# Deferring the gate columns of an input projection: one sample group or three

## The chip, the cores and the metric

The kernel runs on one core of one Trainium2 chip. The metric is the time of one execution on the device in microseconds (us), the median over several runs; lower is better. One further execution is taken with the hardware profiler, and all rows below come from it.

## The reference

One layer of a bidirectional encoder is applied to a prompt of 256 tokens and to a sample of 2048 tokens, all in float32 with a model width of 1024. The part that matters here:

```python
h = _rmsnorm(x, prm['norm_mix'][l])
p = h @ prm['w_in'][l]
pg, pr, ps = _split(p, [GLA_COLS, RWKV_COLS, SSD_COLS])
o_gla = _gla_mixer(pg, ...)
o_rwkv = _rwkv7_mixer(pr, ...)
o_ssd = _ssd_mixer(ps, ...)
mix = jnp.concatenate([o_gla, o_rwkv, o_ssd], axis=-1)
x = x + mix @ prm['w_out'][l]
h = _rmsnorm(x, prm['norm_ffn'][l])
x = x + (jax.nn.silu(h @ prm['ffn_gate'][l]) * (h @ prm['ffn_up'][l])) @ prm['ffn_down'][l]
```

Each of the three token mixers runs a scan forward over the tokens and a second one backward, and sums them. Two of them end with a gate: the first multiplies by `silu(g)`, where `g` is 256 columns of `p`, and the third by `silu(z)`, where `z` is 512 columns of `p`. No scan needs these 768 columns. They are the gate columns of this text.

## The kernel before, in words

**Tiling.** Tokens are handled in groups of 512 (`GS`) for dense work and in blocks of 256 (`TB`) for the mixers. The prompt is one group of one block. The sample is four groups, called group 0 to group 3 here, that start at tokens 256, 768, 1280 and 1792 of the joint axis.

**The projection.** `in_proj` makes one group's columns of `p` and stores them to DRAM. It begins with `normed`, which calls `norm_T` for each of the four 128-token tiles: one DMA loads the rows into a tile `x` (two buffers), ScalarE squares them, VectorE works out the inverse root and scales, TensorE transposes in eight steps of 128 x 128, and ScalarE and VectorE split the result into a high and a low part. These are the two tiles `hT0` and `hT1`, of which there is one buffer each. `normed` runs at a raised priority (`high_priority(offset=3000)`). Then follow the steps of `in_proj`, with a `yield` behind each: four of `in_chan` for the RWKV columns, one for small columns, four for the SSD convolution channels, one for the GLA queries and keys, one of `in_tok` for the GLA values. `in_gates` makes the gate columns in three more steps: one `in_chan` (256 columns, result by channel, matmuls with 512 tokens moving) and two `in_tok` (256 columns each, result by token, 256 columns moving). Each step loads a weight panel of 1024 x 256 in four DMAs on SP's queue, splits it into a high part on ScalarE and a low part on VectorE or GpSimd (`panel`), and multiplies three times per tile of the contraction (`acc3`: high by high, high by low, low by high).

`in_proj` has a flag `part`: 2 makes all columns, 0 leaves the gate columns out, 1 makes the gate columns alone. With 1 the whole `normed` is done again, since `hT` has been overwritten by then.

**The passes.** `pass_a` is the forward scan of one block (and what the backward one can be given in advance), nine in all. `first(end)` emits those first passes whose inputs are there. `pass_b` is the backward scan of one block and needs the gate columns of its block: it reads `d_gl` and `d_z` from DRAM. `second(t0, n)` emits a group's second passes from the last block to the first, each followed by `out_proj`. `ffn` is the feed-forward of one group and needs `hT` again.

**Order.** `run` writes the order of emission out by hand, and a scheduler then orders the instructions of each engine by this order (as priority) and a simulated timeline. Work that is emitted later fills an engine where earlier work isn't ready. Inside one engine instructions run in the order found. In `run`, for each sample group: the projection without gate columns, the first passes that have become possible, then the group's gate steps. Group 0 leaves its gate steps out, and these are made behind the loop. Then come two steps of the prompt's `ffn`, and then, going from group 3 down to group 0, second passes and `ffn` in alternation. `order` is the list of sample groups from the last to the first.

The line that the change touches in the loop, and the two behind it:

```python
dense = self.in_proj(t0, n, 2 if k or len(sample) == 1 else 0)
...
if len(sample) > 1:
    emit(self.in_proj(*sample[0], 1))
```

Of the kernel before, what the change touches and what calls it, by code (L numbers as in the profile page):

```python
# [69 lines left out]
class Encoder:  # L70
# [1029 lines left out]
    def run(self):  # L1100
        self.setup()
        prompt = [(t, min(GS, self.Lp - t)) for t in range(0, self.Lp, GS)]
        sample = [(t, min(GS, self.NT - t)) for t in range(self.Lp, self.NT, GS)]
        done, st, sb, self.rs2, self.ready = 0, None, None, {}, {}

        def first(end):

            nonlocal done, st
            while done < self.NB:
                lo, hi = self.seq(done)  # L1110
                need = (done + 1) * TB
                if need > end or (need == end and need != hi):
                    break
                if done * TB == lo:
                    st = self.states()
                self.pass_a(done, st)
                done += 1

        def second(t0, n):

            nonlocal sb
            mix = None
            for b in range((t0 + n) // TB - 1, t0 // TB - 1, -1):
                if (b + 1) * TB == self.seq(b)[1]:
                    sb = self.states()
                if mix is not None:
                    self.out_proj(b + 1, mix)
                mix = self.pass_b(b, sb)
                self.free = False
                yield  # L1130
            self.out_proj(t0 // TB, mix)

        def run(*steps):

            steps = list(steps)
            while steps:
                for s, k in list(steps):
                    for _ in range(k):
                        if next(s, steps) is steps:
                            steps.remove((s, k))  # L1140
                            break

        def emit(steps, k=None):
            while (k is None or k > 0) and next(steps, steps) is not steps:
                k = k and k - 1

        order = sample[::-1]
        self.last = order[0][0]
        for t0, n in prompt:
            emit(self.in_proj(t0, n))  # L1150
            if t0 == 0:
                self.setup_mixers()
            first(t0 + n)
        ahead = [second(*g) for g in reversed(prompt)]
        for k, (t0, n) in enumerate(sample):
            dense = self.in_proj(t0, n, 2 if k or len(sample) == 1 else 0)
            if k == 1 or k == len(sample) - 1:
                for s in ahead:
                    emit(s, 1)
                    emit(dense, 5)  # L1160
                    emit(s)
                ahead = []
                first(t0)
            if k > 0 or len(sample) == 1:
                emit(dense, 11)
                first(t0 + n)
            emit(dense)
        if len(sample) > 1:
            emit(self.in_proj(*sample[0], 1))
        early = [self.ffn(*g, inside=g[1] <= TB) for g in prompt]  # L1170
        for f in early:
            emit(f, 2)
        rest = [self.ffn(*g, after) for g, after in zip(order, order[1:] + [None])]
        for k, f in enumerate(early + rest):
            steps = [(second(*order[k]), 1)] if k < len(order) else []
            run(*steps, (f, 2))
# [30 lines left out]
```

## Time and profile before

| What | us |
|---|---|
| median of 3 runs | 3870.42 |
| lowest and highest run | 3868.07, 3875.63 |
| the profiled execution, its own time | 3868.33 |
| its span in the trace | 3866.6 |

The span reaches from the first to the last instruction of the program. TensorE's matmuls are called PE in the profile, its weight loads PEld, VectorE is DVE, ScalarE is ACT, GpSimd is POOL and SyncE, on whose queue most DMAs are issued, is SP. The granted clock (PEclk) is TensorE's clock as a share of full speed. Matmuls are pipelined, and their ends in the trace are modelled, so the time from one start to the next is the better measure for a row of equal matmuls. In a row of a group, "mean ns" is that of one instruction.

### The profile page before, as it was taken

How to read it: one execution, taken by the hardware profiler on the slowest of the kernel's cores; microseconds unless marked ns; L12 is line 12 of the kernel's file. 1: busy time of each engine (PE TensorE's matmuls, PEld its weight loads, DVE VectorE, ACT ScalarE, POOL GpSimd, SP SyncE). 2: the span in 40 equal slices, each digit the busy share in tenths (PEclk: the TensorE clock that was granted, in tenths of full speed). 3: DMA queues.
4: the chain of work that ended last, by engine and by line, in shares of the span. 5: the costliest groups of instructions: out<-in, count | busy, mean ns of one | idle time of the engine just before them, and what ended most of it. 6: DMA issues, size and time to landing. Idle time of an engine off the chain costs nothing.

```text
span 3866.6 us, 74228 instructions
## 1 busy us (share of the span) xinstructions
PE 3670.0 (95%) x28958; PEld 3100.1 (80%) x28958; DVE 2414.1 (62%) x5551; ACT 1488.2 (38%) x3354; POOL 614.3 (16%) x636
## 2 busy tenths in 40 slices
PE   6899899899989988999999999999999999999998
PEld 6777677667767767798978888888888888888887
DVE  5943486776884788677756564574654755545444
ACT  4533253544553454443433232333233332333222
POOL 3321123342432332211000000010000000000000
PEclk9999899999989989999999999999999999999999
DMA  6543343333334432555544333434343442434232
GB/s 179 165 142 112 95 151 118 105 121 112 118 98 116 134 104 92 159 158 169 179 149 136 108 122 123 142 116 131 105 142 103 144 131 88 141 104 136 93 99 93
DMA packets 430190, 486.44 MB, mean 126 GB/s; under 512 B 49345, under 2 KB 389457, under 8 KB 428689
## 3 DMA queue, kind: packets, MB, share of 16 engines
q1 hardware_dynamic: 390720, 422.40, 35.8%
q10 hardware_dynamic: 38112, 55.65, 4.0%
q8 instruction: 228, 3.74, 0.4%
q0 software_dynamic: 1008, 3.67, 0.3%
q14 instruction: 122, 0.99, 0.1%
HBM read 395.42 MB, written 86.18 MB: 125 GB/s over the span
## 4 chain that ended last, share of the span: by engine, by line
PE 78%; DVE 12%; DMA 5%; ACT 2%; issue 2%; POOL 0%; SPq 0%; ACTq 0%; DVEq 0%; POOLq 0%
PE d L116 48%; PE g L116 15%; PE s L116 7%; PE a L116 4%; PE c L116 3%; DVE mix L102 2%; DMA mix<-d_xb 1%; DVE wl L92 1%; DVE mix L92 1%; PE d L362 1%; ACT mix L105 1%; DMA b<-d_rk 1%; DMA x<-d_x 0%; DVE b9x L102 0%; PE s L587 0%
## 5 line engine op out<-in xcount | busy, mean ns | idle before, releaser
L116 PE MATMUL d<-hT,wh 128*128 128x512 f32 (+3 forms) x4384 | 1268.0, 374 | 6.2 <-ACT ev L109 2.5
L109 ACT ACTIVATE wh<-wr 128x512 fp32r<-128x512 f32 (+1 forms) x1084 | 624.0, 621 | 981.9 <-PE d L116 587.1
L116 PEld LDWEIGHTS d<-hT,wh 128*128 128x128 f32 (+1 forms) x4384 | 786.8, 191 | 156.9 <-issue 10.8
L92 DVE TENSOR_TENSOR wl<-wr,wh 128x512 fp32r<-128x512 f32 x944 | 646.6, 712 | 360.8 <-ACT wh L109 354.4
L116 PE MATMUL d<-hT,wl 128*128 128x512 f32 (+3 forms) x2192 | 812.1, 374 | 13.1 <-DVE wl L92 13.1
L116 PEld LDWEIGHTS d<-hT,wl 128*128 128x128 f32 (+1 forms) x2192 | 416.0, 190 | 92.1 <-DVE wl L92 15.1
L116 PE MATMUL g<-hT,wh 128*128 128x512 f32 x896 | 284.5, 394 | 0.2 <-ACT hT L109 0.2
L92 POOL TENSOR_TENSOR wl<-wr,wh 128x512 fp32r<-128x512 f32 (+1 forms) x140 | 209.7, 1500 | 451.6 <-ACT wh L109 350.9
L116 PE MATMUL d<-wh,b 128*128 128x256 f32 x928 | 266.8, 289 | 2.4 <-DVE b4d L92 2.0
L116 PE MATMUL d<-wh,hT 128*128 128x256 f32 x1216 | 253.4, 299 | 12.8 <-ACT wh L109 5.9
L116 PE MATMUL d<-wl,b 128*128 128x256 f32 x928 | 260.5, 282 | 0.0
L116 PE MATMUL d<-wh,b9x 128*128 128x256 f32 x928 | 259.5, 283 | 0.0
L116 PEld LDWEIGHTS d<-wh,hT 128*128 128x128 f32 x1216 | 201.7, 198 | 26.6 <-ACT wh L109 7.2
L116 PEld LDWEIGHTS g<-hT,wh 128*128 128x128 f32 x896 | 166.6, 188 | 35.3 <-ACT hT L109 0.5
L116 PE MATMUL d<-wl,hT 128*128 128x256 f32 x608 | 180.3, 298 | 11.5 <-DVE wl L92 11.3
L116 PEld LDWEIGHTS d<-wh,b 128*128 128x128 f32 x928 | 174.3, 188 | 8.9 <-DVE b4d L92 2.2
L116 PE MATMUL d<-wh,mix 128*128 128x256 f32 x832 | 169.8, 292 | 7.0 <-ACT mix L109 2.2
L116 PE MATMUL g<-hT,wl 128*128 128x512 f32 x448 | 175.4, 392 | 0.0
L116 PEld LDWEIGHTS d<-wl,b 128*128 128x128 f32 x928 | 174.8, 188 | 0.7
L116 PEld LDWEIGHTS d<-wh,b9x 128*128 128x128 f32 x928 | 174.0, 189 | 1.3
L102 DVE SCALAR_TENSOR_TENSOR mix<-mix,cwh,mix 128x256 f32<-128x256 f32 x288 | 136.3, 521 | 18.9 <-ACT mix L105 18.9
L116 PEld LDWEIGHTS d<-wh,mix 128*128 128x128 f32 x832 | 136.9, 195 | 10.0 <-ACT mix L109 2.9
(387 smaller groups left out, 6429.3 us busy)
## 6 DMA issues: line engine op xcount, KB each, us to landing
wr<-in_w_in SPq DMA_DIRECT2D x260, 256.0 KB, 3.2
wr<-in_ffn_gate SPq DMA_DIRECT2D x220, 256.0 KB, 2.9
wr<-in_ffn_up SPq DMA_DIRECT2D x220, 256.0 KB, 3.0
wr<-in_ffn_down SPq DMA_DIRECT2D x220, 256.0 KB, 2.9
wr<-in_w_out SPq DMA_DIRECT2D x144, 256.0 KB, 3.0
x<-in_x_sample SPq DMA_DIRECT2D x20, 512.0 KB, 3.7
x<-d_x SPq DMA_DIRECT2D x20, 512.0 KB, 4.3
q_s<-qs ACTq DMA_DIRECT2D x18, 520.0 KB, 4.4
```

Of the source, the lines that this page charges most:

```text
L92: (eng or self.nc.vector).tensor_tensor(out=out, in0=a, in1=b, op=op)
L102: (eng or self.nc.vector).scalar_tensor_tensor(out=out, in0=a, scalar=s, in1=b, op0=op0, op1=op1)
L105: self.nc.scalar.activation(out=out, in_=in_, func=f, **k)
L109: self.nc.scalar.activation(out=out, in_=in_, func=AF.Copy)
L116: self.nc.tensor.matmul(out, lhsT=lhsT, rhs=rhs, start=start, stop=stop, tile_position=tp, skip_group_check=lax)
L362: self.nc.tensor.transpose(ps[:, k * P:(k + 1) * P], h[:, (4 * q + k) * P:(4 * q + k + 1) * P], self.c["ident"])
```

## The change

The flag becomes 0 for all sample groups but the last. Behind the loop the gate columns of groups 2, 1 and 0 are made in this order, each with its own `normed`. Group 3's gate steps stay where they were, and so do those of the prompt.

```diff
         for k, (t0, n) in enumerate(sample):
-            dense = self.in_proj(t0, n, 2 if k or len(sample) == 1 else 0)
+            dense = self.in_proj(t0, n, 2 if k == len(sample) - 1 else 0)
             if k == 1 or k == len(sample) - 1:
@@
             emit(dense)
-        if len(sample) > 1:
-            emit(self.in_proj(*sample[0], 1))
+        for g in order[1:]:
+            emit(self.in_proj(*g, 1))
         early = [self.ffn(*g, inside=g[1] <= TB) for g in prompt]
```

## Rows read from the trace of the kernel before

**Rows 1.** The page: busy time and share of the span of each engine

```profile
PE 3670.0 (95%) x28958; PEld 3100.1 (80%) x28958; DVE 2414.1 (62%) x5551; ACT 1488.2 (38%) x3354; POOL 614.3 (16%) x636
```

**Rows 2.** The page: the chain that ended last, by engine

```profile
PE 78%; DVE 12%; DMA 5%; ACT 2%; issue 2%; POOL 0%; SPq 0%; ACTq 0%; DVEq 0%; POOLq 0%
```

**Rows 3.** Busy time by stage: length; PE, PEld, DVE, ACT, POOL; clock, DMA, GB/s

```profile
652.00:960.00 308.00, 291.93 (x2394) 224.01 (x2395) 214.78 (x476) 144.73 (x341) 103.81 (x102) 0.97 0.38 119
960.00:1304.00 344.00, 317.29 (x2597) 250.72 (x2597) 240.97 (x529) 152.63 (x356) 108.83 (x106) 0.95 0.38 117
1304.00:1562.00 258.00, 233.13 (x2230) 184.28 (x2229) 207.26 (x438) 135.89 (x320) 91.53 (x101) 0.93 0.32 101
1562.00:2000.00 438.00, 415.61 (x4494) 377.94 (x4493) 307.14 (x766) 184.92 (x439) 50.78 (x58) 0.97 0.54 168
2000.00:3866.00 1866.00, 1844.14 (x12892) 1599.34 (x12891) 1046.68 (x2415) 593.38 (x1255) 78.04 (x87) 1.00 0.38 118
```

**Rows 4.** SP's timeline: start, length, the last value stores of groups 1 to 3

```profile
652.22 0.42 SPq L407 DMA_DIRECT2D d_v<-ev  x1
...
960.08 9.72 SPq L407 DMA_DIRECT2D d_v<-ev  x4
...
1299.19 10.25 SPq L407 DMA_DIRECT2D d_v<-ev  x4
```

**Rows 5.** TensorE's timeline: start, length; matmuls 256 wide, four transposes, matmuls 512 wide

```profile
347.87 0.28 PE L116 MATMUL d<-wl,hT 128*128 128x256 f32 x1
...
348.23 0.28 PE L116 MATMUL d<-wl,hT 128*128 128x256 f32 x1
...
348.82 0.60 PE L362 MATMUL d<-ident,x 128*128 128x128 f32 x4
...
381.33 0.39 PE L116 MATMUL d<-hT,wl 128*128 128x512 f32 x1
...
382.01 0.39 PE L116 MATMUL d<-hT,wl 128*128 128x512 f32 x1
```

**Rows 6.** Busy time of the matmuls on hT alone: length, PE, clock, DMA, GB/s

```profile
652.00:700.00 48.00, 36.97 (x238) 0.97 0.55 169
```

**Rows 7.** Busy time of all engines where the gates of groups 1 and 2 stand

```profile
652.00:700.00 48.00, 48.00 (x350) 43.49 (x350) 24.89 (x61) 14.77 (x30) 13.65 (x14) 0.97 0.55 169
960.00:1083.00 123.00, 111.24 (x1081) 89.10 (x1082) 107.49 (x216) 64.36 (x147) 50.02 (x48) 0.98 0.33 105
```

**Rows 8.** Groups of instructions by form, VectorE, then ScalarE: what the norm issues

```profile
L92 DVE TENSOR_TENSOR hT<-d,hT 128x512 fp32r<-128x512 f32 x80 | 54.1, 682 | 21.5 <-ACT hT L109 21.4
L102 DVE SCALAR_TENSOR_TENSOR x<-x,rx,gain 128x1024 f32<-128x1024 f32 x22 | 28.9, 1317 | 0.1
L102 DVE SCALAR_TENSOR_TENSOR rx<-rx 128x1 f32<-128x1 f32 x66 | 12.9, 208 | 0.3
...
L109 ACT ACTIVATE hT<-d 128x512 fp32r<-128x512 f32 x80 | 46.2, 591 | 41.7 <-PE d L362 32.0 <-DMA cw<-in_ssd_conv_w 7.0 <-issue 1.3
L105 ACT ACTIVATE junk<-x 128x256 bf16<-128x256 f32 x96 | 39.7, 413 | 21.7 <-DMA x<-in_x_sample 7.8 <-DVE x L92 4.6 <-issue 3.8
```

**Rows 9.** DMA issues: count, KB each, median us to landing

```profile
x<-in_x_sample SPq DMA_DIRECT2D x20, 512.0 KB, 3.7
```

**Rows 10.** Waits of SP's queue, 652 to 1562 us: total, times, longest

```profile
SPq L353 <- PE d L362: 31.8, 11, 6.0
```

**Rows 11.** Busy time of all engines in five gaps between users of hT

```profile
700.00:753.00 53.00, 43.00 (x475) 31.05 (x472) 45.22 (x115) 38.02 (x110) 22.26 (x22) 0.90 0.24 80
1083.00:1123.00 40.00, 33.34 (x244) 25.47 (x241) 35.74 (x83) 23.70 (x64) 15.89 (x17) 0.80 0.35 117
1422.00:1472.00 50.00, 42.38 (x415) 30.70 (x415) 45.55 (x101) 31.99 (x83) 17.86 (x24) 0.89 0.39 128
1562.00:1590.00 28.00, 23.28 (x261) 20.31 (x260) 22.19 (x48) 16.25 (x39) 9.38 (x12) 0.88 0.66 214
1780.00:1820.00 40.00, 38.16 (x395) 34.85 (x396) 24.82 (x53) 16.48 (x44) 4.68 (x5) 0.91 0.55 169
```

## The prediction

> **What bounds the kernel now.** I read the share of each engine first, then the chain that ended last, then the busy time by stage, and last the two places where the moved work stands today. TensorE is busy 95% of the span and VectorE 62% [rows 1], and TensorE holds 78% of the chain, VectorE 12% [rows 2]. So TensorE bounds the kernel on the whole. By stage this is not even [rows 3]. The first two rows there are the periods of sample groups 1 and 2 (the last value stores of the in-projection of groups 1, 2 and 3 leave near 652, 970 and 1309 us [rows 4]), the third is the last first passes, the fourth the first second passes, the fifth the rest. TensorE is idle 16, 27, 25, 22 and 22 us in them. From 652 to 1562 us it is idle 68 us of 910; in the 1866 us behind 2000 only 22. VectorE is busy 70%, 70%, 80%, 70% and 56%. So whatever is added behind the last first pass lengthens the run by its full TensorE time, while what is taken out ahead of it returns its TensorE time only as far as TensorE is what the passes wait for there. That difference is what this forecast is about.
>
> **What is moved, and its size.** The gate columns of one group are 2 x 24 matmuls 512 wide (one panel) and 2 panels x 4 token blocks x 24 = 192 matmuls 256 wide. Three of the first kind stand 0.68 us from start to start, 0.227 each; three of the second 0.36 us, 0.12 each [rows 5]. That makes 48 x 0.227 + 192 x 0.12 = 10.9 + 23.0 = 33.9 us for a group, 67.8 us for the two that move. The trace agrees: from 652 to 700 us, behind group 1's projection, 238 matmuls on hT are recorded, 37.0 us busy [rows 6].
>
> **What comes back ahead of the last first pass.** Group 1's gates stand in a stretch in which TensorE is busy 48.0 of 48 us and VectorE 24.9 [rows 7]: TensorE is the bound, and I count the full 33.9. Group 2's gates are threaded through first passes from 960 to 1083 us: TensorE is busy 111.2 of 123, VectorE 107.5 [rows 7]. There I count 33.9 x 111.2/123 = 30.7, as the rest of that time a pass was the bound. Together 64.6 us back. The bounds: 33.9 if group 2's stretch is set by the passes alone and nothing comes back there, and 2 x 48 = 96 if the passes run freely as soon as no gate matmul stands ahead of theirs in TensorE's queue. I am nearer to the middle, because TensorE is at 90% or more in both rows.
>
> The Trainium skill (Perfetto Trace Analysis, section Identifying the Most-Contended Engine) says that matmul busy time is a poor measure of TensorE's headroom and that the share of weight loads is a better one. Here that share is 73% in the first two stages and 86% in the last [rows 3], so by that rule 67.8 x 0.73/0.86 = 57.6 us would come back instead of 64.6, and the time would be 7 us longer than my sum. I keep to busy time, because the largest gaps are accounted for below.
>
> **What is added behind it.** The 67.8 us of matmuls, whole: after 1562 us TensorE is busy 95% and then 99% [rows 3].
> Then hT has to be made again, once for each of the two groups, since it has one buffer and group 3 has overwritten it. Per group: 32 transposes, four of which take 0.60 us [rows 5], so 4.8 us, 9.6 for two. On VectorE 8 subtractions of 0.682, 4 scalings of 1.317 and 52 small steps of some 0.21 [rows 8]: 21.6 us; on ScalarE 8 copies of 0.591 and 16 squares of 0.413 [rows 8]: 11.3 us. I cost these at nothing, for they run while TensorE has second passes and the output projection to do: VectorE is 70% and ScalarE 42% busy from 1562 to 2000 us [rows 3]. Without that cover they are the gap priced next. The DMAs: 4 loads of 512 KB a group, 3.7 us each [rows 9], eight in all, 4 MB in a stage that moves 168 GB/s with the engines 54% busy [rows 3]; nothing. They go through SP's queue, where the third and fourth wait until transposes free one of the two x buffers: 11 such waits took 31.8 us, at most 6.0 [rows 10]. Behind a waiting load stand the weight panels of these gates and the loads of the second pass; at worst 4 x 6 us on TensorE's path, inside the same gap. The panel loads, their ScalarE copies and the subtractions on VectorE and GpSimd are moved, not added; GpSimd loses work in the stages where it is a third busy and gets it where it is 12% busy [rows 3].
>
> **The gap.** Between two users of hT no dense matmul can run: the old one must be read, four x blocks loaded, normed, transposed, split. Five such gaps are in the trace [rows 11]: 53, 40, 50, 28 and 40 us long, with TensorE idle 10.0, 6.7, 7.6, 4.7 and 1.8 us, the granted clock (of the two levels 1.2 and 2.4 GHz) 0.80 to 0.91 on the mean. The change makes two more. Today two gaps lie ahead of 1304 us and one (group 0's gates) in the last passes; those stay, with group 2's gates in the place of group 0's. The two new ones fall behind the last first pass, and the rows nearest to that place are 4.7 and 1.8, the two behind 1562 us: 3.3 each, 6.6 us. Bounds: 2 x 1.8 = 3.6 and 2 x 10.0 = 20; on the upper side the lower clock can take another 2 x 0.1 x 34 = 7.
> The gain of the feed-forward, one load on GpSimd's queue, goes behind group 0's gates as today. The feed-forward of the prompt needs hT as well and is late next: it starts at about 1562 us, and will now start after two more sets of gates. The second pass of the last group needs only group 3's gates, which stay, so it can start as before and covers the gaps.
>
> **The sum.** 67.8 + 9.6 + 6.6 - 64.6 = +19.4 us. The profiled execution took 3868.3 us (span 3866.6), so 3887.7; the median of the runs, 3870.4, is 2.1 higher. I take 3889 us, 0.5% slower. A measurement of this kernel can tell 0.2%, about 8 us.
>
> **Rivals.**
> A, faster: the gates are what holds the first passes back. In 652 to 700 us VectorE is busy only 52% while a first pass is under way [rows 7]; the pass's small matmuls sit in order behind gate matmuls. If this is the bound, both stretches give back some 48 us rather than 34, and the norm of the next group runs under a pass. Then 67.8 + 9.6 + 3.6 - 96 = -15, 3855 us. It decides if the next first pass starts over 40 us earlier for each group. Against it: from 960 to 1083 us VectorE is already 87% busy, so there is little to free.
> B, no difference: all dense work is one stock which any pass can draw on. Then 67.8 come back, the transposes fall into idle time, the gaps are covered by second passes: between 0 and +7, about 3873 us. For it speaks that the projection of the next group can stand in for the gates at once; against it that it can't during the gap, which now follows the projection directly.
> C, much slower: the passes lose their cover. In group 2's stretch VectorE is the bound (87%), and without gates TensorE simply idles: 33.9 come back, the gaps cost 20: 67.8 + 9.6 + 20 - 33.9 = +63.5, 3934 us.
> For C speaks the Trainium skill (Perfetto Trace Analysis, section Optimization Strategy): a kernel of several regimes gains by interleaving them. This change takes TensorE work out of a stretch with VectorE at 87% and puts it mostly where VectorE is at 70% or less; the rule's full cost would be that of C.
> That the work would not move at all is excluded: with the flag at 0 the generator ends before the gates.
>
> **Chances and range.** My forecast 0.45, A 0.20, B 0.17, C 0.18. So faster by over 0.2%: 0.20; within: 0.17; slower: 0.63. The range reaches from 3850, below A's price, to 3926, which leaves out the upper part of C. As A has the other sign: the forecast's own range is 3880 to 3905.
>
> **What would show it.** In the changed profile TensorE's matmul count is 64 higher and its busy time about 10 us longer, less what overlaps. Group 2's first projection matmuls should start near 719 us instead of 753, the last projection of group 3 should end near 1240 instead of 1304 us. Two more groups of four x loads stand behind it, each followed by gate stores. The last first pass should end near 1500. Behind it the prompt's feed-forward should start about 84 us later than that shift alone would give. If the projection of group 3 ends at 1270 or later, C is right; at 1210 or earlier, A. If the two new gaps have TensorE idle over 8 us each, my price for them was wrong. What would make the forecast wrong most easily is the order that the scheduler finds: it is made anew for the whole program, and idle time of some 10 us in any stage can come or go with it.

## The result, and the profile after

The changed kernel takes 3898.9 us in the median, against 3869.2 for the kernel before in the same session: a ratio of 1.0074, 95% interval 1.0060 to 1.0088. It is slower by 30 us, as forecast in sign and nearly in size (3889 was forecast, 3850 to 3926 the range). The way there was another than the one in the sum, and most of this section and the next is about that. The profiled execution spans 3890.1 us, 23.5 more than that of before.

The page of the changed kernel, the engines' busy time and the chain by engine, which answer to [rows 1, 2]:

```profile
span 3890.1 us, 74595 instructions
PE 3687.8 (95%) x29022; PEld 3113.4 (80%) x29022; DVE 2459.4 (63%) x5679; ACT 1513.6 (39%) x3434; POOL 613.6 (16%) x636
...
PE 78%; DVE 12%; DMA 6%; ACT 2%; issue 2%; SPq 0%; POOL 0%; ACTq 0%; DVEq 0%; POOLq 0%
```

TensorE has 64 matmuls more, the transposes of two groups, and is busy 17.8 us longer; its idle time went from 196.6 to 202.3 us. So on the page the whole loss is 17.8 us of work and 5.7 of waiting. The stages tell more. Busy time by stage in the changed kernel, cut at the same events as [rows 3] (columns as there); the fourth line is new, from the last first pass's store of its state to the first load of the rows that the prompt's feed-forward adds to, a stretch that before had no length:

```profile
650.00:918.00 268.00, 254.26 (x2105) 192.61 (x2106) 205.83 (x452) 135.59 (x320) 89.41 (x94) 0.96 0.38 120
918.00:1204.00 286.00, 267.10 (x2279) 201.58 (x2278) 217.48 (x469) 140.83 (x332) 96.37 (x96) 0.96 0.36 115
1204.00:1482.00 278.00, 246.12 (x2306) 198.12 (x2306) 237.68 (x542) 148.67 (x363) 102.03 (x108) 0.91 0.33 105
1482.00:1644.00 162.00, 142.50 (x1411) 122.19 (x1412) 89.76 (x228) 57.89 (x148) 36.27 (x40) 0.87 0.44 139
1644.00:2026.00 382.00, 368.72 (x3712) 337.69 (x3713) 264.54 (x654) 160.84 (x370) 28.34 (x30) 0.98 0.54 169
2026.00:3890.00 1864.00, 1842.30 (x12862) 1598.46 (x12858) 1047.11 (x2411) 592.75 (x1254) 78.02 (x87) 1.00 0.37 119
```

SP's timeline of the changed kernel, the last value stores of groups 1 to 3, which answer to [rows 4] (start, length):

```profile
650.54 0.42 SPq L407 DMA_DIRECT2D d_v<-ev  x1
...
928.24 0.40 SPq L407 DMA_DIRECT2D d_v<-ev  x1
...
1202.42 8.24 SPq L407 DMA_DIRECT2D d_v<-ev  x4
```

Group 3's projection is done 99 us earlier than before: its last value stores end at 1211 instead of 1309 us. The sum had 64.6 for what comes back ahead. How much earlier the last first pass ends depends on the store that is looked at. ScalarE's queue, before and then in the changed kernel, the last store of the third mixer's state and the last store of all, the second mixer's values:

```profile
1580.34 0.33 ACTq L925 DMA_DIRECT2D q_s<-qs  x1
...
1587.27 0.46 ACTq L550 DMA_DIRECT2D q_v<-UV  x1
```

```profile
1481.98 0.33 ACTq L925 DMA_DIRECT2D q_s<-qs  x1
...
1529.64 0.46 ACTq L550 DMA_DIRECT2D q_v<-UV  x1
```

The state is stored 98 us earlier, the values only 58. The stage boundary at 1482 us above is the first of the two. The prompt's feed-forward, which comes behind the last gates, loads these rows at 1644 instead of 1562 us, 82 later; this load is the mark for its start here. From that point on the second pass of group 3, which ran beside the gates, is ahead, and the next stage is shorter (382 us against 438). The last stage is as long as before, 1864 against 1866 us.

The gaps between users of hT in the changed kernel, the three behind group 3's projection (columns as in [rows 11]):

```profile
1309.00:1354.00 45.00, 33.59 (x241) 26.37 (x240) 44.22 (x115) 29.41 (x78) 15.63 (x17) 0.69 0.33 109
1443.00:1497.00 54.00, 42.62 (x329) 32.90 (x324) 46.32 (x111) 26.81 (x73) 20.92 (x21) 0.81 0.33 114
1567.00:1598.00 31.00, 19.09 (x186) 15.35 (x185) 25.73 (x72) 12.00 (x35) 11.33 (x13) 0.64 0.43 136
```

In the first two no gate matmul runs (the 0.05 us are the end of the one before); what touches hT are the steps on VectorE and ScalarE that make it (the instructions on hT alone: PE, PEld, DVE, ACT; clock, DMA, GB/s):

```profile
1309.00:1354.00 45.00, 0.05 (x1) 0.00 (x0) 5.36 (x8) 4.66 (x8) 0.69 0.33 109
1443.00:1497.00 54.00, 0.00 (x0) 0.00 (x0) 4.44 (x7) 4.39 (x8) 0.81 0.33 114
```

TensorE is idle 11.4, 11.4 and 11.9 us in the three gaps, and the mean granted clock is 0.69, 0.81 and 0.64: for a good part of each gap the clock was at 1.2 instead of 2.4 GHz. Before, group 0's gap had 7.6 us idle at 0.89, and those behind it 4.7 and 1.8 [rows 11].

The Trainium skill (TensorE: Matmul & The Clock Gate, section HAM oscillation) says that a TensorE which idles between bursts has its clock gated down and begins the next burst slow. The three rows above agree, with 0.64 to 0.81.

### The profile page after: what moved, and what is told of

It is laid out like the page before. It is cut to its first block, busy times and chain, and to the rows that moved or that the text cites. A ratio compares the mean times of both kernels' runs of the same rounds, so it can differ in the third digit from the quotient of the medians.

```text
span 3890.1 us, 74595 instructions
## 1 busy us (share of the span) xinstructions
PE 3687.8 (95%) x29022; PEld 3113.4 (80%) x29022; DVE 2459.4 (63%) x5679; ACT 1513.6 (39%) x3434; POOL 613.6 (16%) x636
## 4 chain that ended last, share of the span: by engine, by line
PE 78%; DVE 12%; DMA 6%; ACT 2%; issue 2%; SPq 0%; POOL 0%; ACTq 0%; DVEq 0%; POOLq 0%
PE d L116 48%; PE g L116 15%; PE s L116 7%; PE a L116 4%; PE c L116 3%; DVE mix L102 2%; DMA mix<-d_xb 1%; DVE wl L92 1%; DMA x<-in_x_sample 1%; PE d L362 1%; DVE mix L92 1%; DMA x<-d_x 1%; ACT junk L105 1%; DVE b4a L92 0%; PE s L587 0%
## 5 line engine op out<-in xcount | busy, mean ns | idle before, releaser
L116 PE MATMUL d<-hT,wl 128*128 128x512 f32 (+3 forms) x2192 | 814.4, 375 | 17.9 <-DVE wl L92 17.8
L116 PE MATMUL g<-wh,b 128*128 128x256 f32 x480 | 138.7, 289 | 4.3 <-DVE b4a L92 3.0
```

Of the source, the lines that this page charges most:

```text
L116: self.nc.tensor.matmul(out, lhsT=lhsT, rhs=rhs, start=start, stop=stop, tile_position=tp, skip_group_check=lax)
```

## The experiments

Three theories were put to the test. Theory 1: what costs is making hT again, and moving the gates is free. Theory 2: the first passes lose their cover. Theory 3: moving the gates frees the first passes (rival A's mechanism), and remaking hT takes that back and more. All ratios below are against the kernel before, timed beside each run, which makes the runs of different sessions comparable; 0.1% is 3.9 us.

**Gates from the hT that is there (e1).** Groups 2 and 1 take their deferred gates from group 3's hT:

```diff
-        hT = self.normed(t0, n, self.gain("norm_mix"), lambda t: self.xrow(t)[0])
-        if part == 1:
+        hT = self.kept if part == 3 else self.normed(t0, n, self.gain("norm_mix"), lambda t: self.xrow(t)[0])
+        self.kept = hT
+        if part in (1, 3):
...
-            emit(self.in_proj(*g, 1))
+            emit(self.in_proj(*g, 1 if g[0] == self.Lp else 3))
```

> The changed kernel, but the gates of groups 2 and 1 behind the last first pass are multiplied from the hT that group 3 left, without loading, norming and transposing the rows again (so those gate columns are made from other rows; the matmuls, panels and stores are all there). Theory 1 (what costs is making hT again: transposes, gap and lower clock; moving the gates is free): back at the time before, 3869 within 8. Theory 2 (the first passes lose their cover and TensorE idles): the loss stays, 3890 or more. Theory 3 (moving the gates frees the first passes, as rival A had it, and the gap gives it back): below the kernel before, near 3842.

Measured: 3835.3 us, ratio 0.9913 (0.9899 to 0.9926). Theory 3's number was 3842. Remaking hT for two groups costs 1.61% of the time of before, 62 us, 31 a group, where the sum had 4.8 for the transposes and 3.3 for the gap. And the moving alone, far from free, gains 0.87%, 34 us. Theories 1 and 2 fall. The page of this kernel, and its busy time from the end of group 3's projection to the prompt's feed-forward, in two stages:

```profile
span 3828.2 us, 74191 instructions
PE 3662.1 (96%) x28958; PEld 3088.9 (81%) x28958; DVE 2420.2 (63%) x5551; ACT 1490.3 (39%) x3354; POOL 615.6 (16%) x636
```

```profile
1196.00:1482.00 286.00, 266.53 (x2496) 214.24 (x2495) 229.71 (x476) 141.73 (x319) 108.70 (x114) 0.95 0.33 106
1482.00:1577.00 95.00, 90.65 (x1044) 76.80 (x1043) 55.70 (x138) 38.60 (x100) 25.22 (x31) 0.98 0.48 154
```

The last first pass stores its state at 1482 us in both kernels (its last store of all leaves at 1507 us here and at 1530 in the change). But here the feed-forward follows 95 us after the state instead of 162, TensorE's idle time in both stages together is 23.8 us instead of 51.4, and the clock is 0.95 and 0.98 instead of 0.91 and 0.87. The two stages do not hold the same work in both kernels (3540 matmuls here, 3717 in the change), so what the 62 us consist of is read from the whole spans, which differ by 64 matmuls, the transposes. The change is idle 202.3 us against 166.1, which is 36 of the 62, and busy 25.7 us longer. Of the latter 9.6 are the transposes, and the rest, 16, I put down to the lower clock.

**Which groups are deferred (e2, e3, e4).** Only the set of groups is changed:

```diff
-            dense = self.in_proj(t0, n, 2 if k == len(sample) - 1 else 0)
+            dense = self.in_proj(t0, n, 0 if k in (0, 2) else 2)
...
-        for g in order[1:]:
+        for g in (sample[2], sample[0]):
```

That is e2; e3 has `(0, 1)` and `(sample[1], sample[0])`, e4 has the flag at 2 for all groups and no loop behind.

> Gates deferred for groups 0 and 2 only; group 1 makes its own in place. Theory 1: one remaking of hT more than before, half of the loss, 3884. Theory 2: group 2's gates stand where VectorE is 87% busy, so nearly the whole loss is here, 3895. Theory 3: between, as the return ahead (some 48 us) and the gap behind come as a pair, 3884.

> Gates deferred for groups 0 and 1 only; group 2 makes its own in place. Theory 1 and theory 3: half of the loss, 3884. Theory 2: group 1's gates stand where TensorE is 100% busy and VectorE 52%, so little is lost, 3873.

> No gates deferred at all: every group makes its own in place, hT is remade for none. Theory 1: one remaking less than the kernel before, 3869 - 14 = 3855. Theory 2: the last first passes lose group 0's gates as cover, 3869 to 3890. Theory 3: 14 us are saved on the remaking and the first passes of groups 1 and 2 stay as they are: 3855 to 3869.

Measured: groups 0 and 2 3880.1 us, 1.0028 (1.0014 to 1.0042); groups 0 and 1 3863.3 us, 0.9983 (0.9974 to 0.9992); none 3854.7 us, 0.9958 (0.9946 to 0.9970). The last is what theory 1 had, and theory 3 allowed. The two in the middle differ: deferring group 1 gains a little, deferring group 2 loses. By theory 1 both would be 3884; the order is that of theory 2, each 10 to 15 us lower, though e1 takes away its reason. So the cost isn't a fixed sum per group; it hangs on where the remaking falls. Deferring both (1.0074) costs more than the two changes by themselves would add up to (-0.17% and +0.28%).

**The second pass ahead (e5).** The first step of group 3's second pass is emitted before the gates of groups 1 and 0:

```diff
+        late = second(*order[0])
-        for g in order[1:]:
+        for k, g in enumerate(order[1:]):
+            if k == 1:
+                emit(late, 1)
             emit(self.in_proj(*g, 1))
...
-            steps = [(second(*order[k]), 1)] if k < len(order) else []
+            steps = [(second(*order[k]) if k else late, 1)] if k < len(order) else []
```

> The changed kernel, with the first step of group 3's second pass emitted ahead of the gates of groups 1 and 0, so that it has the higher priority and can fill TensorE in the two gaps behind the last first pass. If the gaps are long for want of other work (cover): a good part of the some 36 us of idle that remaking hT costs comes back, 3875 to 3885. If the chain of norm and transposes is itself held up by the second pass on VectorE: 3899 or more.

Measured: 3910.1 us, 1.0091 (1.0073 to 1.0108), not better than the change (the intervals overlap). Busy time of all engines in the two new gaps of this kernel:

```profile
1440.00:1493.00 53.00, 41.68 (x333) 32.32 (x331) 46.59 (x111) 26.82 (x72) 21.44 (x22) 0.84 0.34 116
1567.00:1603.00 36.00, 24.63 (x245) 19.98 (x245) 28.40 (x86) 15.74 (x43) 12.18 (x12) 0.67 0.54 169
```

TensorE idles in them as it does in the change. The cover that I had counted on in the forecast did not come with more priority for the second pass. But the first loads of that pass moved only from 1473 to 1470 us, so what ran beside the first of these gaps is nearly the same in both kernels; another way of covering it isn't excluded.

**The kernel before, without remaking (e6), and the change without any (e11).** In e6 the one line behind the loop is `emit(self.in_proj(*sample[0], 3))`, with the edit of `in_proj` as in e1; in e11 all three groups of the change take flag 3.

> The kernel before, with group 0's gates multiplied from the hT that group 3 left instead of remaking it (so those gate columns are made from other rows). If one remaking costs the same wherever it stands, 32 us: 3837. If it costs what was forecast for a gap, 8 us: 3861. If it costs what leaving group 0's gates in place has given, 15 us: 3854.

> As e1, and group 0's gates too are multiplied from group 3's hT, so that nothing is remade (gate columns of groups 0, 1 and 2 made from other rows). Beside the kernel before without remaking (e6, 0.9945 of before) it shows what moving the gates of groups 1 and 2 does by itself. If moving gains what e1 showed: 0.983 to 0.987 of before, 3803 to 3820. If the gain in e1 came from group 0's remaking falling in a better place: 3845 or more.

Measured: e6 3853.1 us, 0.9945 (0.9926 to 0.9963); e11 3824.8 us, 0.9883 (0.9867 to 0.9900). e11 lies just above the 0.983 to 0.987 that was expected. So with nothing remade on either side, moving the gates of groups 1 and 2 behind the last first pass gains 0.62%, 24 us. And by the ratios a remaking is worth 21 us in the kernel before (e6; its 3853 is close to the 3854 expected for 15 us, but the kernel before took 3872.5 in that session), some 12 for the last of three in the change (e11 against e1, whose intervals just touch), 31 each for the other two (e1 against the change).

**Work or standstill: e8, e9, e10.** All of the remaking's work is done beside e1, for nobody:

```diff
+        if part == 3:
+            self.normed(t0, n, self.gain("norm_mix"), lambda t: self.xrow(t)[0], ghost=True)
...
+            if hT is None:
+                ev = [self.hp.tile([P, GS], F32, tag="ev", name="ev", bufs=3)[:].rearrange("p (k n) -> p k n", k=4) for _ in range(2)]
+                self.copy(ev[0], v, "a")
+                self.tt(ev[1], v, ev[0], ALU.subtract)
+                return
```

> As e1 (gates of groups 2 and 1 multiplied from the hT that group 3 left), but with all of the remaking's work done beside it: loads, squares, scaling, transposes and the split, whose results go to scratch tiles that nobody reads (so those gate columns are made from other rows). If the cost of remaking is its work on the engines: 3890 to 3899 as in the changed kernel. If it is the gap, that is, that no gate matmul can run meanwhile: near 3835 + 10 us for the 64 transposes = 3845.

Measured: 3901.4 us, 1.0061 (1.0040 to 1.0082), as slow as the change. By what was written before it, the work is to blame. But the trace shows that the run didn't take the gap away. Busy time of the matmuls on hT alone in this kernel, in the two stretches where the ghost's transposes stand:

```profile
1317.00:1360.00 43.00, 0.00 (x0) 0.00 (x0) 0.00 (x0) 0.00 (x0) 0.70 0.34 106
1467.00:1517.00 50.00, 0.00 (x0) 0.00 (x0) 0.00 (x0) 0.00 (x0) 0.76 0.45 149
```

Not one gate matmul runs in them, although hT is ready and nobody waits for the ghost's results. Their weight panel isn't what is missing: no panel is split between 1324 and 1360 or between 1475 and 1517 us, so the one that the first gate matmuls behind the stretches read was ready 36 and 42 us before. The norm has the raised priority, so its transposes stand ahead of the gate matmuls in TensorE's order, and both use the same ring of two PSUM buffers; which of the two holds the gates back wasn't separated. The clock is 0.70 and 0.76 as in the change. So e8 alone leaves the question open; it needs the two halves. In e9 the ghost has no transposes and no split, in e10 no squares, root and scaling:

```diff
         def half(q):
+            if hT is None:
+                return
             ps = self.ps(self.dps, "d")
```

```diff
-        if rs is None:
-            rs = self.inv_rms(h[:], "rx")
-        self.stt(h[:], h[:], rs, g, ALU.mult, ALU.mult)
+        if hT is not None:
+            if rs is None:
+                rs = self.inv_rms(h[:], "rx")
+            self.stt(h[:], h[:], rs, g, ALU.mult, ALU.mult)
```

> As e1 (gates of groups 2 and 1 multiplied from the hT that group 3 left), with the loads, squares, root and scaling of the remaking done beside it for nobody (ScalarE and VectorE work, of VectorE some 16 us a group), but no transposes and no split. If it is the work on VectorE that costs: 3870 to 3885. If it is that gate matmuls stand still behind the transposes (which they did in e8 too, where nothing of the data asked for it: the gate matmuls came behind the transposes in TensorE's order): near 3835, at most 3850.

> As e8, with the loads, transposes and split done for nobody, but without squares, root and scaling, so that the transposes wait for the load alone (gate columns of groups 2 and 1 made from other rows, as in e1). If the work on VectorE costs (here 5.5 us a group): about 3850. If any transposes ahead of the gates cost, the chain in front of them being only part of it: 3860 to 3880. If it is the length of the chain from load to transpose that holds the gates back: 3845.

Measured: e9 3827.7 us, 0.9885 (0.9868 to 0.9903); e10 3872.9 us, 1.0002 (0.9992 to 1.0013). Where e9 does the work on VectorE and ScalarE, it costs nothing that could be measured at the end: e9 is 0.28% below e1, not slower, and the intervals just touch. But it is another place. Without transposes the scheduler put the ghost's loads earlier, from 989 to 1083 us, into first passes; VectorE isn't idler there (busy 92% to 95%), and group 3's last value store leaves at 1214 us against 1202 in e1, which the rest of the run makes up. With transposes and split, and only the loads in front of them, the run is 0.89% longer than e1: 34 of the 62 us of loss are there again. Busy time of e9 and then of e10, from group 3's last value stores to the feed-forward:

```profile
1203.00:1573.00 370.00, 350.55 (x3506) 286.30 (x3501) 280.30 (x592) 181.43 (x420) 131.78 (x141) 0.97 0.39 122
```

```profile
1204.00:1628.00 424.00, 382.88 (x3716) 312.64 (x3715) 316.06 (x684) 197.30 (x464) 140.90 (x148) 0.93 0.39 121
```

VectorE does 280 and 316 us of work in them, TensorE idles 19.5 and 41.1, and the clock is 0.97 and 0.93. The instructions on hT alone in e10, in the two stretches where its transposes stand (columns as in the lines on hT of the change):

```profile
1309.00:1342.00 33.00, 0.00 (x0) 0.00 (x0) 0.00 (x0) 0.00 (x0) 0.85 0.34 103
1450.00:1480.00 30.00, 0.00 (x0) 0.00 (x0) 0.00 (x0) 0.00 (x0) 0.89 0.47 152
```

So the loss goes with the time in which the dense matmuls on hT stand still while rows are brought to TensorE and turned: 33 and 30 us in e10 (34 us lost against e1), 43 and 50 in e8 (57 lost), 45 and 54 in the change (62 lost). In e1 and e9 there is no such stretch at these two places. What isn't separated is the norm's work on VectorE at these very places, which e8 has and e10 hasn't, from the longer standstill that comes with it.

**hT kept in DRAM (e7).** hT of groups 0 to 2 is stored when it is made and loaded slice by slice for the gates:

```diff
-        hT = self.normed(t0, n, self.gain("norm_mix"), lambda t: self.xrow(t)[0])
+        if part == 1:
+            hT = self.new_hT()
+            with self.tc.high_priority(offset=3000):
+                for k in range(KD):
+                    for i in range(2):
+                        self.nc.sync.dma_start(out=hT[i][:, k].bitcast(F32), in_=self.saved[t0][i][:, k])
+        else:
+            hT = self.normed(t0, n, self.gain("norm_mix"), lambda t: self.xrow(t)[0])
+        if part == 0:
+            self.saved[t0] = [self.dr.tile([P, KD, GS], F32, name=f"d_h{i}_{t0}", tag=f"d_h{i}_{t0}") for i in range(2)]
+            for i in range(2):
+                self.nc.sync.dma_start(out=self.saved[t0][i][:], in_=hT[i][:].bitcast(F32))
```

> The changed kernel, but hT of groups 0, 1 and 2 is stored to DRAM when it is made (4 MB each) and loaded again slice by slice for the deferred gates, instead of loading, norming and transposing. The gap stays in a shorter form (a slice has to land), VectorE, ScalarE and transposes have no part in it. If the cost of remaking is the gap's length: about 10 us a group, 3835 + 2 x 10 - 22 for group 0 = 3833. If it is the missing filler in itself, the gap however short: 3870 or more. If the 24 MB more on the DMA queues collide with the passes' loads: over 3880.

Measured: 3846.8 us, 0.9931 (0.9914 to 0.9947). It computes the whole of the reference, and is 0.7% faster than the kernel before and 1.4% faster than the change. The matmuls on hT alone in this kernel, right behind group 3's last z stores (columns as in the lines on hT of the change):

```profile
1339.00:1360.00 21.00, 10.75 (x41) 7.36 (x41) 0.00 (x0) 0.00 (x0) 1.00 0.64 226
```

In the change no such matmul ran for 45 us at this place. Here they run for half of these 21 us, at a full clock, while the slices land (DMA 64% busy). Against e11, which remakes nothing, the three reloads cost 0.48%, 19 us, some 6 a group. The forecast of 3833 was too low, above all because group 0's remaking was worth 12 us and not 32.

## Why the prediction was right

The sign and the size came out because two terms were wrong in opposite directions, by 34 and 38 us (the sum itself gives 3889.8, not 3889). That they nearly cancelled was luck.

**What is moved** was right: 64 more matmuls are the transposes, no others, and all the moved gates run behind group 3's projection. They run beside the last first passes, not behind them: those of group 2 begin at 1354 us.

**What comes back ahead** was put at 64.6 us, TensorE's time of the gates times its share in each stretch. Group 3's projection, ahead of which two sets of gates are gone and nothing is added, ended 99 us earlier. That is rival A's bound of 96, and the mark that I had set for A (group 3's projection done at 1210 or earlier) was reached, if narrowly: its last value stores leave from 1202 to 1211 us. From the end of one group's value stores to the next it was 318 and 340 us before [rows 4] and is 278 and 282 now, 40 and 58 less, each more than the 34 us of matmuls that were taken out. The step that failed is the one that took TensorE's own time for what comes back (33.9 + 30.7) and left anything more to A. I put the rest down to the first pass being a chain of small steps, which goes faster by more than the matmuls' own time with 240 dense matmuls fewer among them. A part of the 99 us is only put off: the two stages hold 607 matmuls fewer [rows 3], of which 480 are the gates, and the other 127 are nearly all small ones of the passes, which now come later. That VectorE was 87% busy in group 2's stretch, my reason against A, didn't hinder it. e11 against e6 shows that this gain is real at the end of the run too: 24 us.

By the rule of the Trainium skill on weight loads (Perfetto Trace Analysis, section Identifying the Most-Contended Engine) less should have come back than by busy time, 57.6 us. The measured 99 is on the other side of both. The same page (section Optimization Strategy) says that interleaving different regimes may help, which spoke for rival C; at this place it doesn't: e11 against e6 gains 0.62% by taking TensorE work out of the stretch with the busy VectorE.

**What is added behind** was 67.8 + 9.6 + 6.6 = 84 us. From the end of group 3's projection to the end of the run it was 2679 us instead of 2557, 122 more. The term that was mis-sized is the gap: with its transposes a remaking costs 31 us (e1) where I had 4.8 + 3.3 = 8.1. I took the two rows nearest by place, 4.7 and 1.8 us idle, and the trace of before shows that neither is a gap of the kind that the change adds. The instructions on hT alone in these two stretches (columns as in the lines on hT of the change):

```profile
1562.00:1590.00 28.00, 9.83 (x53) 8.09 (x53) 2.02 (x3) 1.67 (x3) 0.88 0.66 214
1780.00:1820.00 40.00, 0.00 (x0) 0.00 (x0) 0.00 (x0) 0.00 (x0) 0.91 0.55 169
```

In the first, the end of hT being made for the prompt's 256 tokens, 53 matmuls on hT run. In the second hT isn't made at all, and the output projection's dense matmuls fill TensorE. The three gaps of before in which hT was made for 512 tokens had 10.0, 6.7 and 7.6 us idle [rows 11]; the new ones have 11.4 and 11.9, above even the 10.0 that I had as the upper bound and over the 8 us each that I had named as the sign of a wrong price. In them there were only first and second passes, and these leave TensorE both idle and at a low clock. The clock, which I had as an afterthought of 7 us in the upper bound, is nearly half as large as the idle time: over the whole span the change has 36 us more idle and, transposes aside, 16 us more busy time than e1.

**What I costed at nothing**, the work on VectorE and ScalarE, wasn't seen to cost anything where e9 did it; at the place where the remaking stands it wasn't measured apart from the standstill. In the first new gap VectorE is busy 44.2 of 45 us, so its work may well set the length of the gap there.

**The rivals.** A's mechanism was there, but its price behind was too low; B (dense work is one stock) is refuted by e1 and e11, which differ from before by far more than 7 us; C's loss of cover didn't show ahead, and what resembles it, a TensorE without cover, occurred behind.

What stays open: how the 31 us divide into idle time and clock in each gap, and why group 1 alone is cheap to defer and group 2 is not. The order of all engines is made anew for each variant. e9 against e1, 0.28% lower with more work, suggests that differences of this size between variants can come from that alone, so e2 and e3 shouldn't be read closer. A second buffer for hT, 32 KB a partition more, would be the direct test of the standstill; it wasn't tried.

## What to carry to other kernels

Where work is deferred, price what has to be made again by how long the bounding engine goes without its dense stream, not by how much work the making is: here 31 us for some 5 us of transposes. In this kernel the operand that had to come back was cheaper loaded from DRAM than made anew through the bounding engine, even at 4 MB a group. Before a row of the trace is taken as the price of a gap, look whether the thing to be made is made in it. And if a forecast sums a gain and a loss of like size, check both by marks in the trace: the sum here was right while each half was off by 34 to 38 us.

## What was not expected of the hardware and its order

A transpose that nobody waits for holds back dense matmuls that are ready: in e8 no gate matmul ran for 43 and 50 us. TensorE's clock falls to a mean of 0.64 to 0.81 in stretches in which the trace shows it busy 62% to 79% of the time, as the small matmuls of the passes come with waits between them. And storing 12 MB and loading them again beside running passes cost only some 19 us in all.
